# Sums of w_out split in other units of a Hymba block, with the first pair's gate products earlier on GpSimd

## The chip, the cores and the metric

The kernel runs on one core of a Trainium2 chip, alone. The metric is the time of one execution in device microseconds; three runs of the kernel before gave 958.17, 953.5 and 954.65 us, median 954.65. A profiled execution took 958.72 us, of which the profile's span is 956.9 us. Engines are named as in the profile: PE (TensorE matmul), PEld (its weight loads), DVE (VectorE), ACT (ScalarE), POOL (GpSimd), SP (the queue that issues the DMAs).

## The reference

One layer of a hybrid encoder. 16 meta tokens are prepended to a prompt of 256 tokens and to a sample of 2048; both go through the same layer in float32 (model width 1024).

```python
h = rmsnorm(z, norm_w)
proj = einsum('bld,de->ble', h, w_in)             # 1024 -> 2816
q, k, v, g_att, c_val, c_glu, g_conv = split(proj)
q = rmsnorm(q per head, q_norm_w); k = rmsnorm(k per head, k_norm_w)
att = windowed_gqa(q, k, v, sink) * silu(g_att)   # window 128, ALiBi, meta keys, sink
u = c_val * sigmoid(c_glu)
cnv = silu(layernorm(depthwise_conv31(u))) * silu(g_conv)
out = z + concat([att, cnv]) @ w_out              # 1024 -> 1024
```

## The kernel before

**Exact float32 by parts.** A float32 matrix product is made of three passes over parts of the operands: hi times hi, hi times lo and lo times hi. ACT casts the hi part and DVE subtracts it to get the lo part. Every weight and every activation that feeds PE goes through such a split.

**Stages.** The 2304 tokens and the 16 meta tokens are six groups of columns in two chunks of three groups. The input projection runs over eleven weight units of 256 columns, in the same order for each chunk: four conv units (U_C, value and gate), two units of the conv gate (U_GC), two of the attention gate (U_GA), one K/V unit (U_KV) and two Q units (U_Q). One unit and one group make PSUM tiles `pj`, each of 24 matmuls (L1020 for conv and gates, L1036 for K/V and Q). For K, GpSimd makes a reciprocal root (L179, L180), DVE multiplies it in (`kn`, L1194) and so frees the pj tile; PE transposes (`kt`). For Q, DVE makes `qs` (L1167) in the same way. SP loads the next activations `xt`, DVE scales them (L929), ACT and DVE or GpSimd split them into `xh` and `xl` (L948, L958).

**The depthwise convolution** is 31 taps for each conv unit and chunk, each one DVE instruction of 128x1167 (L1103). A planner meters them: `tick` gives PE time as credit, `owe` takes credit for other DVE work, and taps are issued from a queue while credit lasts. When all taps of a chunk are out, and LN_WAIT further steps of the planner's clock have gone by, its layer norms (`ln_block`) are issued.

**The output weights** w_out are needed as hi and lo rows and as sums and differences of rows (a product scheme that saves multiplications). `presplit_wo(e)` splits one row block and `presplit_sums(i)` makes one of two sets of seven operands: a cast on ACT (L394), a subtraction on DVE (L395), five more subtractions (L400) and seven stores of 512 KB to a DRAM buffer `wod`. The raw rows lie in four buffers of tag `xt`, which the activations use too, the operands in two of tag `xn`. `split_at` (L1347 to L1354) says beside which unit and group each of them is issued; `later(k)` puts a step k planner steps on.

**Attention and output.** The 18 blocks of 128 tokens are handled in steps of eight slots: scores S (L469), bias and maximum on DVE (L527), exponentials on ACT (L539), a normalisation on POOL (`pm` L556, `sb` L565), transposes of the probabilities on PE (`pT`, L585, L581), copies to `ptiles`, the product with V (`O`, L619). Blocks are paired for the output projection (`yb`, L725), whose operands are parts and sums of gated attention and gated convolution. `acts` (L758 to L781) lists for a pair p at which slot the gate tiles are loaded (`load_mix`: gc and cn, L446 and L448), when GpSimd multiplies them (`mix_conv`, L699), and when the parts are made (`two_parts`, L683 and L684). The first slots are spread through the last two Q units of chunk 1 (`spread`). `q_prep(a)` transposes the queries of block a (slot QSLOT = 6 of the step before).

**Order.** A scheduler orders each engine's queue, except those under a manual order: POOL from the opening of attention on (MAN1) and PE too in the rest (MAN2) keep the order in which the program is written. Each queue runs in its order; an instruction that waits holds all behind it. The pieces of w_out are loaded from `wod` (L438) into tiles that take over the buffers of xh and xl: wo0 and wo1 those of group 3, wo2 and wo3 those of group 4, which pj146 to pj148 read last.

Of the kernel before, what the change touches and what calls it, by code (L numbers as in the profile page):

```python
# [24 lines left out]
NB = NB_P + NB_S  # L25
# [20 lines left out]
CACHE = 2  # L46
WST = 9
W0 = 3
LN_WAIT = (9, 1)
LTAGS = "dbdbd" + "dcdcddddd"  # L50
LTAGS_N = len(LTAGS)
MAN1 = {mybir.EngineType.Pool}
# [1 line left out]
QSLOT = 6  # L54
# [27 lines left out]
NS = 2  # L82
# [34 lines left out]
CHUNKS = [[0, 1, 2], [3, 4, 5]]  # L117
U_C = [0, 1, 2, 3]
U_GC = [4, 5]
U_Q = [6, 7]  # L120
U_KV = 8
U_GA = [9, 10]
# [8 lines left out]
def hymba_kernel(  # L131
# [58 lines left out]
    def owe(ns):  # L190
        credit[0] -= ns

    def later(k, f):
        due.setdefault(clock[0] + k, []).append(f)
# [87 lines left out]
    vt, qt, q2t, sbt, pmt, gat, gct, cnt, att, opj = ({} for _ in range(10))  # L282
# [40 lines left out]
    vt, qt, q2t, sbt, pmt, gat, gct, cnt, att, opj = ({} for _ in range(10))  # L323
# [37 lines left out]
    def presplit_wo(e):  # L361

        raw = [sp.tile([P, 2, 400], F32, tag="xt", name=f"wor{e}_{nh}", bufs=XTB)[:, :, :UW] for nh in range(2)]
        for nh in range(2):
            src = w_out[e][:, 512 * nh : 512 * nh + 512].rearrange("p (a n) -> p a n", n=UW)
            nc.sync.dma_start(raw[nh], src)

        def split():
            hi = sp.tile([P, D], F32R, tag="xn", name=f"wohi{e}")
            if e < 4:  # L370
                owe(700)
            to = [wod[PIECES_W.index((e, hl))] for hl in range(2)]
            for nh in range(2):
                part = hi[:, 512 * nh : 512 * nh + 512].rearrange("p (a n) -> p a n", n=UW)
                nc.scalar.copy(part, raw[nh])
                nc.vector.tensor_tensor(raw[nh].bitcast(F32R), raw[nh], part, op=ALU.subtract)
                dst = to[1][:, 512 * nh : 512 * nh + 512].rearrange("p (a n) -> p a n", n=UW)
                later(1, lambda nh=nh, dst=dst: nc.sync.dma_start(dst, raw[nh]))
            later(1, lambda: nc.sync.dma_start(to[0], hi.bitcast(F32)))

        later(2, split)

    def presplit_sums(i):

        raw = {}
        for key, e, nh in ((11, 4 + i, 0), (21, i, 0), (12, 4 + i, 1), (22, i, 1)):
            raw[key] = sp.tile([P, 2, 400], F32, tag="xt", name=f"wor{key}_{i}", bufs=XTB)[:, :, :UW]
            src = w_out[e][:, 512 * nh : 512 * nh + 512].rearrange("p (a n) -> p a n", n=UW)
            nc.sync.dma_start(raw[key], src)

        def operand(name, key):
            both = sp.tile([P, D], F32R, tag="xn", name=f"wo{name}_{i}")
            hi, lo = (both[:, 512 * k : 512 * k + 512].rearrange("p (a n) -> p a n", n=UW) for k in range(2))
            nc.scalar.copy(hi, raw[key])  # L394
            nc.vector.tensor_tensor(lo, raw[key], hi, op=ALU.subtract)  # L395
            owe(700)
            later(1, lambda: nc.sync.dma_start(wod[PIECES_W.index((name, i))], both.bitcast(F32)))

        def minus(dst, x, y):
            nc.vector.tensor_tensor(raw[dst], raw[x], raw[y], op=ALU.subtract)  # L400
            owe(700)

        steps = (
            ("c1", 11, None),
            ("t1", 21, (11, 12, 11)),
            ("s4", 22, (12, 22, 12)),
            ("s1", 11, (22, 22, 11)),
            ("s3", 12, (21, 21, 22)),
            ("s2", 22, None),
            ("t0", 21, None),  # L410
        )

        def step(name, key, diff):
            operand(name, key)
            if diff:
                minus(*diff)

        for k, args in enumerate(steps):
            later(2 + k, lambda args=args: step(*args))
# [24 lines left out]
    def load_mix(b):  # L444
        gct[b] = pool["b"].tile([P, 4, P], F32, tag="gc", name=f"gc{b}", bufs=2)
        nc.sync.dma_start(gct[b], gd[4:8, :, P * b : P * b + P].rearrange("j p n -> p j n"))  # L446
        cnt[b] = pool["b"].tile([P, 4, P], F32, tag="cn", name=f"cn{b}", bufs=2)
        nc.sync.dma_start(cnt[b].rearrange("p j n -> p (j n)"), cd[b])  # L448

    def load_x(p, key):  # L450
        r, nh = key
        rows = NM + P * (2 * p + r)
        tc.keep_in_program_order(nc.sync.dma_start(yo(p, key), z[rows : rows + P, 512 * nh : 512 * nh + 512]))
# [222 lines left out]
    def parts(name):  # L676
        place, k = HOME[name]
        t = cst[place][:, k].rearrange("p (h e n) -> p h e n", h=2, n=P)
        return t[:, 0], t[:, 1]

    def two_parts(name, src):
        hi, lo = parts(name)
        nc.scalar.copy(hi, src)  # L683
        nc.vector.tensor_tensor(lo, src, hi, op=ALU.subtract)  # L684

    def with_rest(f):
        pending.append(f)
        while "rest" in cst and pending:
            pending.pop(0)()
# [8 lines left out]
    def mix_conv(b):  # L698
        nc.gpsimd.tensor_tensor(cnt[b], cnt[b], gct[b], op=ALU.mult)  # L699

    def mix_diff(p):
        nc.gpsimd.tensor_tensor(temp(0), cnt[2 * p + 1][:, 0:NS, :], cnt[2 * p][:, 0:NS, :], op=ALU.subtract)
        diff[p] = True
# [53 lines left out]
    for p in range(NB // 2):  # L757
        b0, b1 = 2 * p, 2 * p + 1  # L758
        for rel, f in (
            (5 - (p == 0), lambda b1=b1: load_mix(b1)),  # L760
            (6 - 2 * (p == 0), lambda b0=b0: load_mix(b0)),
            (9 + 3 * (p == 0), lambda p=p: load_x(p, (0, 1))),
            (11 - 2 * (p == 0), lambda b1=b1: mix_conv(b1)),
            (12 - 2 * (p == 0), lambda b0=b0: mix_conv(b0)),
            (13, lambda p=p: with_rest(lambda: mix_diff(p))),
            (12 + 2 * (p == 0), lambda p=p: load_x(p, (1, 1))),
            (13 - 2 * (p == 0), lambda b1=b1: two_parts("c1", cnt[b1][:, 0:NS, :])),
            (14, lambda: with_rest(lambda: two_parts("s3", temp(0)))),
            (17, lambda b0=b0: two_parts(("c", 0), cnt[b0][:, NS:4, :])),
            (17, lambda p=p: load_x(p, (0, 0))),  # L770
            (20, lambda b1=b1: two_parts(("c", 1), cnt[b1][:, NS:4, :])),
            (18, lambda p=p: load_x(p, (1, 0))),
            (18, lambda p=p: add_kept(p, (1, 1), 0)),
            (20, lambda p=p: add_kept(p, (0, 0), 1)),
            (21, lambda p=p: add_kept(p, (1, 0), 0)),
        ):
            acts.setdefault(16 * p + rel, []).append(f)
        for rel, name, es in JOBS:
            to = late_jobs if name == "s3" else jobs
            rel -= p == 0 and name == "c1"  # L780
            if p == LAST and name in ("t1", (1, 0)):  # L781
                for c0 in (0, 256):
                    to.setdefault(16 * p + rel, []).append((p, name, es, c0, 256))
            else:
                to.setdefault(16 * p + rel, []).append((p, name, es))

    def slot_step(s_, slot):
        a, bb = s_, s_ - 1
        has_a, has_b = a < NB, 0 <= bb < NB
        steps = PLAN if has_b else []  # L790
        if slot == 0:
            if a + 1 < NB:
                load_q(a + 1)
                load_k(a + 1)
        if slot == 1 and has_b and s_ > 1:
            load_ga(bb)
        if slot == VSLOT and 0 < a < NB:
            load_v(a)
        t = 8 * s_ + slot
        with_rest(lambda: None)  # L800
        for f in acts.get(t, ()):
            f()
        if slot < len(steps) and steps[slot]:
            bank(bb, *steps[slot])
        for job in jobs.get(t, ()):
            product(*job)
        if has_a:
            scores(a, slot // 4, slot % 4)
        if slot == QSLOT and a + 1 < NB:
            q_prep(a + 1)  # L810
        for job in late_jobs.get(t, ()):
            product(*job)
        tick(2400)
# [44 lines left out]
    if True:  # L858
# [483 lines left out]
        for n3 in range(3):  # L1342
# [4 lines left out]
        split_at = {  # L1347
            (0, U_C[0], CHUNKS[0][2]): lambda: presplit_wo(6),
            (0, U_C[1], CHUNKS[0][2]): lambda: presplit_wo(7),
            (1, U_C[0], CHUNKS[1][0]): lambda: presplit_wo(2),  # L1350
            (1, U_C[0], CHUNKS[1][2]): lambda: presplit_wo(3),
            (0, U_GA[0], CHUNKS[0][2]): lambda: presplit_sums(0),
            (0, U_KV, CHUNKS[0][0]): lambda: presplit_sums(1),
        }  # L1354

        for i, (c, u, g) in enumerate(items):
# [39 lines left out]
            if (c, u) == (0, ORDER[-1]):  # L1396
                p = preps[g + 3]
# [5 lines left out]
            if i == last_at[c, u] and u == U_GC[-1]:  # L1403
                def ready(c=c):
                    if left[c, 0]:
                        return False
                    seen.setdefault(c, clock[0])
                    return clock[0] >= seen[c] + LN_WAIT[c]

# [68 lines left out]
```

## Time and profile before

| | |
|---|---|
| Median of three runs | 954.65 us (953.5 to 958.17) |
| Profiled execution | 958.72 us |
| Its span | 956.9 us |
| Mean granted TensorE clock | 0.991 |
| DMA moved | 182.80 MB, mean 191 GB/s |

The page gives busy time for each engine and, in 40 slices of 23.9 us, how busy each was; a busy PE is an upper bound since its matmuls are pipelined. The view of waits names, for the waiting engine, the tile that waited and the instruction that released it: total us, times, longest. The windows give busy us and instruction counts of the engines in a stretch, then the granted clock as a share, the DMA share and GB/s. A timeline row has start, duration, engine, line, operation, tiles, shape and count, and in brackets the idle time before it and what ended it. Such rows follow in the prediction, beside the steps that use them.

### The profile page before, as it was taken

The numbers are of one execution on the slowest core, as the hardware profiler recorded it, in microseconds if no ns is written. First come the engines' busy times: TensorE is split into PE (matmuls) and PEld (weight loads), VectorE is DVE, ScalarE is ACT, GpSimd is POOL, SyncE is SP. The second block draws the span as 40 slices with busy tenths as digits, with TensorE's granted clock in tenths as the row PEclk, the third lists the DMA queues.
The fourth block names the chain that finished last, engine by engine and source line by source line (L and its number), as shares of the span: only waits on it lengthen the run. The fifth ranks groups of instructions, "written<-read, shape, count | busy, mean of one in ns | idle before, by whom it ended". The sixth has DMA issues, their size and how long they took to land.

```text
span 956.9 us, 16888 instructions
## 1 busy us (share of the span) xinstructions
PE 935.1 (98%) x5734; PEld 883.2 (92%) x5734; DVE 781.8 (82%) x1340; ACT 448.0 (47%) x1231; POOL 374.0 (39%) x553
## 2 busy tenths in 40 slices
PE   9999999999798999999999999999999999999998
PEld 8999999999698999999999999878888888888887
DVE  5579999988998859999997565668888887897884
ACT  7432112354446761011111346556676776776771
POOL 3320000165758620000000454658665455546554
PEclk9999999999999999999999999989999999999999
DMA  8574345779894642212333687996665665565431
GB/s 294 174 255 186 132 174 182 238 268 338 274 324 155 221 160 104 83 62 110 114 126 138 188 268 246 361 382 180 180 196 158 172 194 173 169 208 162 144 102 46
DMA packets 146342, 182.80 MB, mean 191 GB/s; under 512 B 40944, under 2 KB 106816, under 8 KB 146128
## 3 DMA queue, kind: packets, MB, share of 16 engines
q1 hardware_dynamic: 146256, 181.72, 58.1%
q8 instruction: 45, 0.74, 0.3%
q14 instruction: 41, 0.34, 0.1%
HBM read 115.83 MB, written 65.85 MB: 190 GB/s over the span
## 4 chain that ended last, share of the span: by engine, by line
PE 79%; DMA 7%; DVE 4%; POOL 4%; issue 3%; ACT 2%; SPq 0%; DVEq 0%; POOLq 0%; ACTq 0%
PE pj L1020 36%; PE yb L725 18%; PE pj L1036 8%; PE O L619 5%; PE S L469 4%; DMA xn<-in_z 2%; PE pT_m L585 2%; PE pT_c L585 1%; PE pT_x L585 1%; DMA wod<-wos 1%; DVE y L1103 1%; DVE xt L929 1%; DMA wraw<-in_w_in 1%; DMA xt<-in_zt 1%; PE warmup L1253 1%
## 5 line engine op out<-in xcount | busy, mean ns | idle before, releaser
L1020 PE MATMUL pj<-xh,ws 128*128 128x384 f32 (+1 forms) x1536 | 397.6, 339 | 0.3
L1103 DVE SCALAR_TENSOR_TENSOR y<-us,cw,y 128x1167 f32<-128x1167 f32 x240 | 329.6, 1432 | 0.3
L1020 PEld LDWEIGHTS pj<-xh,ws 128*128 128x128 f32 x1536 | 280.0, 188 | 0.8 <-DVE qs L1167 0.4
L1020 PE MATMUL pj<-xl,ws 128*128 128x384 f32 (+1 forms) x768 | 260.9, 340 | 0.1
L1036 PE MATMUL pj<-ws,xh 128*128 128x256 f32 (+1 forms) x880 | 168.2, 288 | 9.4 <-DVE kn L1194 5.7
L1036 PEld LDWEIGHTS pj<-ws,xh 128*128 128x128 f32 (+1 forms) x880 | 139.8, 191 | 10.7 <-issue 7.4
L1020 PEld LDWEIGHTS pj<-xl,ws 128*128 128x128 f32 x768 | 144.2, 188 | 0.5 <-DVE xl L958 0.4
L725 PE MATMUL yb<-wo,rest 128*128 128x512 f32 (+1 forms) x498 | 132.3, 399 | 0.0
L1036 PE MATMUL pj<-ws,xl 128*128 128x256 f32 (+1 forms) x440 | 126.4, 287 | 0.0
L725 PEld LDWEIGHTS yb<-wo,rest 128*128 128x128 f32 x498 | 87.1, 189 | 15.3
L1128 ACT ACTIVATE go<-pj 128x384 f32<-128x384 f32 x48 | 23.5, 490 | 147.9 <-PE pj L1020 139.5
L539 ACT ACTIVATE sb<-sb,nm 128x304 f32<-128x304 f32 (+5 forms) x144 | 77.8, 541 | 29.6 <-DVE nm L527 27.9
L565 POOL TENSOR_SCALAR sb<-sb,es 128x304 f32<-128x304 f32 (+5 forms) x144 | 73.1, 525 | 38.4 <-PE pT_x L585 18.8
L527 DVE CUSTOM_DVE_ANT_0 sb<-S,bias,vec 128x304 f32<-128x304 f32 (+5 forms) x144 | 74.3, 516 | 15.8 <-PE S L469 14.7
L179 POOL TENSOR_SCALAR ssk<-ssk 128x2 f32<-128x2 f32 x18 | 10.3, 571 | 191.5 <-ACT sqk L1142 191.0
L1036 PEld LDWEIGHTS pj<-ws,xl 128*128 128x128 f32 (+1 forms) x440 | 84.3, 192 | 0.4
L179 POOL TENSOR_SCALAR ssq<-ssq 128x4 f32<-128x4 f32 (+2 forms) x55 | 27.8, 506 | 115.7 <-ACT xn L883 89.5
L469 PE MATMUL S<-kw,q 128*128 128x304 f32 (+5 forms) x288 | 63.5, 302 | 2.8 <-ACT ptiles L601 2.2
L469 PEld LDWEIGHTS S<-kw,q 128*128 128x128 f32 x288 | 52.5, 188 | 13.6 <-ACT ptiles L601 2.4
L725 PE MATMUL yb<-wo,ptiles 128*128 128x512 f32 x216 | 60.8, 411 | 0.0
L647 POOL TENSOR_TENSOR at<-at,ga 128x256 f32<-128x256 f32 x36 | 26.6, 740 | 75.7 <-DVE at L641 75.7
L1063 ACT ACTIVATE sg<-pj 128x384 f32<-128x384 f32 (+1 forms) x24 | 11.8, 493 | 90.3 <-PE pj L1020 81.4
(162 smaller groups left out, 1489.5 us busy)
## 6 DMA issues: line engine op xcount, KB each, us to landing
wd<-ws SPq DMA_DIRECT2D x36, 512.0 KB, 5.8
ws<-wd SPq DMA_DIRECT2D x36, 512.0 KB, 5.7
wraw<-in_w_in SPq DMA_DIRECT2D x52, 256.0 KB, 6.3
xn<-in_z SPq DMA_DIRECT2D x18, 512.0 KB, 5.3
gd<-go SPq DMA_DIRECT2D x48, 192.0 KB, 2.3
wo<-wod SPq DMA_DIRECT2D x18, 512.0 KB, 6.8
yo<-in_z SPq DMA_DIRECT2D x36, 256.0 KB, 3.5
out_y<-yo SPq DMA_DIRECT2D x35, 256.0 KB, 2.5
```

The costliest lines, as they stand in the source:

```text
L179: nc.gpsimd.tensor_scalar(src, src, scale, eps, op0=ALU.mult, op1=ALU.add)
L469: r = f(*a, **k)
L527: nc.vector.tensor_tensor_reduce(out=sb[:, n, c0:c1], in0=ps[:, 0:w], in1=cst["bias"][:, kv, at + c0 : at + c1], scale=1.0, scalar=nsnk[:, ...
L539: nc.scalar.activation(sb[:, n, c0:c1], sb[:, n, c0:c1], AF.Exp, bias=nm[:, n : n + 1], scale=-1.0, accum_out=rs[:, n : n + 1],)
L565: nc.gpsimd.tensor_scalar(sb[:, k, a0:a1], sb[:, k, a0:a1], es[:, k : k + 1], 1.0, op0=ALU.mult, op1=ALU.mult)
L585: nc.tensor.transpose(pt[: c1 - c0, n, :], sbt[b, kv][:, n, c0:c1], ident)
L619: nc.tensor.matmul(opj[b, kv][:, n0:n1], t[:r, kv, :], p[:r, n0:n1], start=(k == "c" and i == 0), stop=(k == "x" and i == len(work) - 1),)
L647: nc.gpsimd.tensor_tensor(at[:, pr, :], at[:, pr, :], gat[b][:, pr, :], op=ALU.mult)
L725: nc.tensor.matmul(ps[:, :n], x[mi][:, i, :], w[wi], start=((name, e) in OPENS and k == 0), stop=(done and e == es[-1] and k == 2), skip_g ...
L1020: nc.tensor.matmul(ps[:, :n], ws[:, d, wi, P * half_i : P * half_i + P], x[xi][:, d, o : o + n], start=(k == 0), stop=(k == 3 * ND - 1),)
L1036: nc.tensor.matmul(ps[:rows, :UW], x[xi][:, d, o : o + rows], ws[:, d, wi, :], start=(k == 0), stop=(k == 3 * ND - 1),)
L1103: nc.vector.scalar_tensor_tensor(y[:, yo + o0 : yo + o1], u[:, o0 + k : o1 + k], cw[:, j, k : k + 1], y[:, yo + o0 : yo + o1], op0=ALU.mul ...
```

## The change

Four things. (1) The planner's wait before the layer norms is 7 instead of 9. (2) For the first pair alone (p == 0) both gate products are written in the same slot as the loads of their operands (slot 4, formerly 9 and 10), and the parts of `c1` two slots sooner. (3) The third q is transposed at slot 3 instead of 6. (4) The row splits 2 and 3 of w_out move from chunk 1's first conv unit to chunk 0's third; the sums' first set moves from chunk 0's first attention-gate unit to its fourth conv unit; the second set from chunk 0's K/V unit to chunk 1's second conv unit.

```diff
-LN_WAIT = (9, 1)
+LN_WAIT = (7, 1)
...
-            (11 - 2 * (p == 0), lambda b1=b1: mix_conv(b1)),
-            (12 - 2 * (p == 0), lambda b0=b0: mix_conv(b0)),
+            (11 - 7 * (p == 0), lambda b1=b1: mix_conv(b1)),
+            (12 - 8 * (p == 0), lambda b0=b0: mix_conv(b0)),
...
-            (13 - 2 * (p == 0), lambda b1=b1: two_parts("c1", cnt[b1][:, 0:NS, :])),
+            (13 - 4 * (p == 0), lambda b1=b1: two_parts("c1", cnt[b1][:, 0:NS, :])),
...
-        if slot == QSLOT and a + 1 < NB:
+        if slot == (3 if s_ == 1 else QSLOT) and a + 1 < NB:
             q_prep(a + 1)
...
-            (1, U_C[0], CHUNKS[1][0]): lambda: presplit_wo(2),
-            (1, U_C[0], CHUNKS[1][2]): lambda: presplit_wo(3),
-            (0, U_GA[0], CHUNKS[0][2]): lambda: presplit_sums(0),
-            (0, U_KV, CHUNKS[0][0]): lambda: presplit_sums(1),
+            (0, U_C[2], CHUNKS[0][0]): lambda: presplit_wo(2),
+            (0, U_C[2], CHUNKS[0][2]): lambda: presplit_wo(3),
+            (0, U_C[3], CHUNKS[0][1]): lambda: presplit_sums(0),
+            (1, U_C[1], CHUNKS[1][0]): lambda: presplit_sums(1),
```

No instruction is added or removed but four more table loads on ACT; the rest is a matter of order.

**ACT at the turn from K/V to Q in chunk 0, before** (wos: an operand of the sums, sqk and sqq: squares for the norms of K and Q, ks: a finished K):

```order
L394 CAST wos4_1_2449<-wor22_1_2259 128x512
L1185 CAST vs8_2548<-pj58_2516 128x2x64
L1142 ACTIVATE sqq0_0_2602,ssq0_0_2601<-pj59_2576 128x64 x2
L394 CAST wos1_1_2502<-wor11_1_2253 128x512
L1142 ACTIVATE sqq0_0_2602,ssq0_0_2601<-pj59_2576 128x64 x2
L1206 ACTIVATE ks5_2460<-kt5_2458,kscale_81 128x128
L1137 ACTIVATE sqq0_1_2651<-pj60_2625 128x256
L1206 ACTIVATE ks6_2512<-kt6_2510,kscale_81 128x128
L394 CAST wos3_1_2552<-wor12_1_2257 128x512
L1142 ACTIVATE sqq0_2_2692,ssq0_2_2691<-pj61_2666 128x64 x4
L394 CAST wos2_1_2611<-wor22_1_2259 128x512
```

The same place after the change:

```order
L1185 CAST vs8_2548<-pj58_2516 128x2x64
L995 CAST ws0_7_2563<-wraw10_3_2570 128x2x256
L1206 ACTIVATE ks5_2463<-kt5_2461,kscale_81 128x128
L1142 ACTIVATE sqq0_0_2598,ssq0_0_2597<-pj59_2572 128x64 x4
L1206 ACTIVATE ks6_2512<-kt6_2510,kscale_81 128x128
L1137 ACTIVATE sqq0_1_2645<-pj60_2619 128x256
L1142 ACTIVATE sqq0_2_2682,ssq0_2_2681<-pj61_2656 128x64 x4
```

The casts of the second set of sums are gone from between the norms of K and Q.

**SP and POOL where attention starts in chunk 1.** SP before: the loads of the gate tiles (gc, cn) of blocks 1 and 0, then the pieces of w_out (wa, wo):

```order
L446 DMA gc1_6235<-gd_64 128x4x128
L226 DMA qd_63<-qr0_17_6173 128x256
L448 DMA cn1_6237<-cd_70 128x512
L446 DMA gc0_6239<-gd_64 128x4x128
L448 DMA cn0_6241<-cd_70 128x512
L428 DMA wa0_6337<-wod_71 128x1024
L442 DMA ga0_6339<-gd_64 128x4x128
L438 DMA wo0_6360<-wod_71 128x1024 x2
```

SP after:

```order
L438 DMA wo0_6362<-wod_71 128x1024 x3
L438 DMA wo1_6409<-wod_71 128x1024
L277 DMA cd_70<-zn17_6135 128x512
L438 DMA wo1_6409<-wod_71 128x1024 x2
L438 DMA wo3_6630<-wod_71 128x1024
L438 DMA wo2_6573<-wod_71 128x1024 x3
L438 DMA wo3_6630<-wod_71 128x1024
L446 DMA gc1_6235<-gd_64 128x4x128
L448 DMA cn1_6237<-cd_70 128x512
L446 DMA gc0_6239<-gd_64 128x4x128
L448 DMA cn0_6241<-cd_70 128x512
```

The four gate loads went from ahead of all wo pieces to behind eleven of them, the last five of which go into the buffers of xh4 and xl4. POOL after the change, at the first normalisation of probabilities (pm, sb), which before had no L699 there (they stood behind the second sb):

```order
L526 MEMSET sb0_5804 128x32
L699 TENSOR_TENSOR cn1_6237<-cn1_6237,gc1_6235 128x512
L699 TENSOR_TENSOR cn0_6241<-cn0_6241,gc0_6239 128x512
L556 TENSOR_TENSOR pm0_0_6253<-sb0_5804,es0_0_6072 128x128
L565 TENSOR_SCALAR sb0_5804<-sb0_5804,es0_0_6072 128x176
L565 TENSOR_SCALAR sb0_5804<-sb0_5804,es0_0_6072 128x208
```

The two products now stand ahead of the first block's normalisation.

**PE at the first transposes of probabilities (pT0), before:**

```order
L1036 MATMUL pj148_6475<-ws1_7_5606,xl4_3258 128x256
L1036 MATMUL pj148_6475<-ws1_7_5606,xh4_3257 128x256 x2
L585 MATMUL pT0_c_0_6447<-ident_72,sb0_5876 128x128
L1036 MATMUL pj148_6475<-ws1_7_5606,xl4_3258 128x256
L1036 MATMUL pj148_6475<-ws1_7_5606,xh4_3257 128x256 x2
L585 MATMUL pT0_c_0_6447<-ident_72,sb0_5876 128x128
```

After:

```order
L1036 MATMUL pj150_6576<-ws1_7_5545,xh5_3500 128x256
L469 MATMUL S1_0_1_6520<-kw1_5796,q2_1_6351 128x240 x2
L469 MATMUL S1_0_2_6565<-kw1_5796,q2_1_6351 128x208 x2
L469 MATMUL S1_0_3_6613<-kw1_5796,q2_1_6351 128x176 x2
L469 MATMUL S1_1_0_6679<-kw1_5796,q2_1_6351 128x272 x2
L469 MATMUL S1_1_1_6698<-kw1_5796,q2_1_6351 128x240 x2
L585 MATMUL pT0_c_0_6449<-ident_72,sb0_5804 128x128
L585 MATMUL pT0_m_0_6515<-ident_72,sb0_5804 128x128
L585 MATMUL pT0_c_0_6449<-ident_72,sb0_5804 128x128
```

Before, the transposes were interleaved with the projection tiles pj148 to pj150; now they stand behind these and behind the second block's scores, and only pj151 is left for later.

## The prediction

> **What bounds the kernel now.** The page's busy line comes first, with the slices of DVE and ACT below it.
>
> ```profile
> PE 935.1 (98%) x5734; PEld 883.2 (92%) x5734; DVE 781.8 (82%) x1340; ACT 448.0 (47%) x1231; POOL 374.0 (39%) x553
> DVE  5579999988998859999997565668888887897884
> ACT  7432112354446761011111346556676776776771
> ```
>
> TensorE leaves some 20 us of the span idle, and no edit takes a matmul away. So the change can win only from those idle microseconds and from time at a reduced clock, and it can lose by making new waits. The view of waits, for PE alone, says who holds it up:
>
> ```profile
> PE pj L1036 <- DVE kn L1194: 5.7, 1, 5.7
> PE pj L1036 <- DVE qs L1167: 3.7, 3, 2.1
> PE S L469 <- ACT ptiles L601: 2.2, 1, 2.2
> PE O L619 <- DVE ptiles L602: 1.6, 1, 1.6
> PE kt L1204 <- DVE kn L1194: 1.4, 1, 1.4
> PE kt-1_2153 L1204 <- DVE kn-1_2102 L1194: 0.5, 1, 0.5
> ```
>
> The kn and qs rows are the K/V and Q units of chunk 0: 7.6 + 3.7 = 11.3 us. The S and O rows (3.8 us) are the first pair of attention blocks. The windows around these places (columns: us; busy and instruction count of PE, PEld, DVE, ACT, POOL; granted clock; DMA share; GB/s):
>
> ```profile
> 225.00:260.00 35.00, 30.73 (x257) 30.05 (x255) 33.30 (x54) 18.15 (x82) 27.01 (x24) 1.00 0.89 297
> 260.00:264.00 4.00, 0.66 (x3) 0.69 (x4) 3.76 (x9) 0.07 (x1) 3.69 (x3) 0.50 1.11 328
> 264.00:268.00 4.00, 4.00 (x26) 4.00 (x26) 4.00 (x6) 0.00 (x0) 2.29 (x2) 0.68 0.87 271
> 315.00:360.00 45.00, 44.85 (x285) 44.19 (x284) 31.09 (x53) 32.58 (x72) 18.22 (x33) 1.00 0.54 188
> 600.00:610.00 10.00, 10.00 (x88) 10.00 (x87) 6.33 (x23) 6.46 (x23) 6.35 (x15) 1.00 1.00 351
> 616.00:620.00 4.00, 2.60 (x20) 2.09 (x18) 3.22 (x10) 2.78 (x10) 4.00 (x5) 1.00 1.09 380
> 620.00:624.00 4.00, 3.42 (x15) 3.12 (x16) 3.12 (x8) 2.27 (x8) 2.99 (x10) 0.70 1.03 406
> ```
>
> In the K/V unit (225 to 260) DVE is busy 33.30 of 35 us; outside it TensorE has full cover. The transition to attention (600 to 632) is the other tight place: PE is full until 610, and DMA runs at its limit of about 390 GB/s.
>
> **The sum's basis.** The profiled execution took 958.72 us (span 956.9); the median of the three runs is 954.65, 0.4% below. I add up differences in the trace and apply them to the median.
>
> **1. The sums leave K/V of chunk 0 (L394, L395, L400 of presplit_sums(1), and sums(0) just before).** The longest wait ends when kn of block 7 is made. The timeline of DVE from kn 6 to kn 7, of ACT, and of POOL there:
>
> ```profile
> 253.56 0.28 DVE L1194 TENSOR_TENSOR kn<-pj,rqk 128x128 f32<-128x128 f32 x1
> ...
> 262.91 0.48 DVE L1194 TENSOR_TENSOR kn<-pj,rqk 128x128 f32<-128x128 f32 x2
> ```
> ```profile
> 259.70 0.37 ACT L1206 ACTIVATE ks<-kt,kscale 128x128 fp32r<-128x128 f32 x1
> 271.23 0.62 ACT L394 CAST wos<-wor 128x512 fp32r<-128x512 f32 x1 [11.16 <-DMA wod<-wos]
> ```
> ```profile
> 255.04 2.71 POOL L179 TENSOR_SCALAR ssk<-ssk 128x2 f32<-128x2 f32 x1 [2.79 <-ACT sqk L1142]
> 257.83 3.57 POOL L180 TENSOR_TENSOR rqk<-ssk,half 128x2 f32<-128x2 f32 x1
> ```
>
> The groups by line from 255 to 315 give the price of a tap and of an L996 (busy us, mean ns):
>
> ```profile
> L1103 DVE SCALAR_TENSOR_TENSOR y<-us,cw,y 128x1167 f32<-128x1167 f32 x14 | 20.0, 1428 | 0.0
> L996 DVE TENSOR_TENSOR ws<-wraw,ws 128x512 fp32r<-128x512 f32 x8 | 5.1, 688 | 0.0
> ```
>
> DVE spends 9.35 us from kn 6 to kn 7, on three taps, four L996, one L400 and two L395 among others. In the new order two taps, three L996 and one L1207 stand there: 2 x 1.43 + 3 x 0.69 + 0.3 = 5.2 us. The 5.7 us wait thus shrinks by 4.1. ACT's 11.16 us stop behind a store of the sums goes too; what is late next is the reciprocal root on POOL, above, which I don't let vanish. Of the other kn waits (1.9) I take away half, 1.0. The half clock from 260 to about 266.5 belongs to the long wait: granted 0.68 in 264:268 means 2.6 us at half speed with PE busy, a loss of 1.3, and 0.3 more before 264: 1.6 goes. Of the qs waits, DVE's loads of xt stood late because the sums held the same ring of four tiles:
>
> ```profile
> L929 DVE SCALAR_TENSOR_TENSOR xt<-xt,vec,bc 128x384 f32<-128x384 f32 x18 | 10.2, 607 | 2.0 <-DMA xt<-in_zt 2.0
> ```
>
> I take 1.3 of 3.7, since the xl work before the longer one stays. **Term: -8.0**, bounds -13 (all 11.3 and the clock) and 0 (the POOL chain alone decides).
>
> **2. Where the sums and presplit_wo(2), (3) go.** Units 2 and 3 of chunk 0 take sums(0) and both row splits, unit 1 of chunk 1 takes sums(1). One sum set is 12 DVE instructions of about 0.68 us, 8.2 us. In chunk 0 taps give way, and DVE's total before Q's end falls by sums(1). In 315:360 DVE has 14 us free, ACT 12. PE has no wait there now, and its pj ring is evacuated by ACT, which is under half busy in slices 4 to 12. **Term: 0**, bounds 0 and +3 (ACT's casts stop behind the stores, as at 271, in front of a sigmoid that frees pj).
>
> **3. The gate products go first on POOL (rel 9, 10 to 4, 4).** POOL follows the written order. Today it works like this:
>
> ```profile
> 603.49 1.74 POOL L565 TENSOR_SCALAR sb<-sb,es 128x176 f32<-128x176 f32 x4
> 605.32 0.19 POOL L179 TENSOR_SCALAR ssq<-ssq 128x4 f32<-128x4 f32 x1
> ...
> 610.40 1.02 POOL L180 TENSOR_TENSOR rqq<-ssq,half 128x4 f32<-128x4 f32 x1
> 613.17 0.40 POOL L556 TENSOR_TENSOR pm<-sb,es 128x128 f32<-128x128 f32 x1 [1.75 <-issue]
> ...
> 616.76 1.27 POOL L699 TENSOR_TENSOR cn<-cn,gc 128x512 f32<-128x512 f32 x1
> 617.97 0.12 POOL L526 MEMSET sb<- 128x32 f32 x1
> 618.06 1.39 POOL L699 TENSOR_TENSOR cn<-cn,gc 128x512 f32<-128x512 f32 x1
> ```
>
> Then the two L699 stand ahead of pm and of the first four L565. They need the loads of gc and cn. In the SP queue these loads stood ahead of all pieces of w_out, and now stand behind eleven of them, the last five of which (wo2, wo3) overwrite xh4 and xl4, so SP waits for pj148, their last reader. The PE rows:
>
> ```profile
> 608.72 0.28 PE L1036 MATMUL pj<-ws,xh 128*128 128x256 f32 x1
> 608.84 0.60 PE L585 MATMUL pT_m<-ident,sb 128*128 128x128 f32 x4
> 626.09 1.55 PE L725 MATMUL yb<-wa,ptiles 128*128 128x512 f32 x6
> 631.16 0.43 PE L469 MATMUL S<-kw,q 128*128 128x176 f32 x2 [2.24 <-ACT ptiles L601]
> ```
>
> I replay it in today's times, where pj148 ends at 609.0. Five pieces of 0.524 MB and four loads of 0.262 MB are 3.67 MB; at 390 GB/s that is 9.4 us, with some 2 us of start and older pieces the last one lands at about 620.6. Products to 622.0, pm and the first L565 to 622.9. PE in its new order has pj149, pj150 and six S pairs before the first pT transpose: 60 matmuls x 0.114 (10.00 us / 88) = 6.8, so it arrives at 615.9 and **waits 7.0 us**. The second sb follows on POOL: rest of the four L565 to 624.3, the four rqq (605.32 to 611.4 today, 6.1 us) to 630.4, pm and L565 to 631.3; PE is back for it at about 627.8 (transposes 1.7, copies of ptiles 1.3, O and qT 1.9) and waits 3.5 again. After that transposes, copy, O, pj151 (2.8) and O once more: yb starts near 638.5 against 626.09, +12.4. The third q, transposed three steps sooner (QSLOT 6 to 3), takes away the 2.24 us wait at 631.16 and its 0.4 us of transposes are done: -2.6. So +9.8, and +0.2 for the clock. **Term: +10**, bounds +3 (PE's wait on POOL is nearly covered, because the loads land as early as today) and +14 (two more stretches at half clock, 1.7 each, and the waits as above). DVE's L684 behind the product stands ahead of two L527 of S1_1, inside the same wait.
>
> By the Trainium skill, "TensorE: Matmul & The Clock Gate", section "What's actually happening", the clock halves after an idle window of about 3.4 us. By that rule the new 7 us wait starts a stretch at half clock that today's waits of 2.24 us at most would not have had, and the sum would, as an estimate, be 1.5 to 3 us higher. The row above says otherwise: 620:624 was granted 0.70 with no wait longer than 1.58 us, so a thin stretch of transposes suffices, the transition pays it already, and I add only 0.2.
>
> **4. LN_WAIT 9 to 7.** In the order the last layer norms stand later all the same, since sums(1) displaces taps in chunk 1, and four table loads more stand on ACT:
>
> ```profile
> L274 ACT ACT_TABLE_LOAD x4 | 5.1, 1283 | 1.1 <-issue 1.1
> ```
>
> 4 x 1.28 = 5.1 us of ACT, which was busy 6.46 of 10 us in 600:610 and holds nothing PE needs within 5 us. **Term: 0**, bounds 0 and +2.
>
> **Sum:** -8.0 + 0 + 10 + 0 = +2.0; 954.65 + 2.0 = 956.7 us.
>
> **Rivals.**
> *The transition has its cover.* If gc and cn land before 610 as today, POOL loses only its 2.7 us of products, and some of that is hidden: term 3 is +1, and 954.65 - 8.0 + 1 = 947.6. For it: the L699 rows of today have no idle time ahead of them. Against: SP's order is fixed and its head waits for pj148. Chance 0.25.
> *The gate products block POOL in full* (slower). The price is decided by the landing of cn: from 616 on each microsecond delays the first transposes by one. With +14, and only the 4.1 and 1.0 won in K/V, 954.65 - 5.1 + 14 = 963.6. For it: SP's head wait. Against: the waits overlap with work at half clock that is paid already. Chance 0.18.
> *The change doesn't do what it says in K/V.* In the order DVE has 27 taps in K/V and Q instead of 23, POOL's 3.57 us root stays beside them, and the wait turns from DVE's queue to POOL: term 1 is -2.5, giving 954.65 - 2.5 + 10 = 962.2. For it: L179 and L180 took 2.71 and 3.57 us there. Chance 0.14. The Trainium skill, "SBUF — State Buffer", section "SBUF: two separate sides", says that a DVE instruction with two SBUF inputs and a GpSimd one that reads SBUF exclude each other for their whole length; the 3.57 us row beside a chain of such DVE rows agrees.
>
> **How the numbers follow.** Forecast 0.43, rivals 0.25, 0.18, 0.14. The forecast's own range is 951 to 962; the first rival reaches down to 945 and the last two up to 965, so the range is 946 to 965. About 0.5% (4.8 us) is what a measurement of this kernel can tell from no change, since its runs differ by that much: faster means below 949.9, slower above 959.4. Faster: the first rival and a little, 0.26. Slower: the last two and a tenth of the whole from the forecast's upper part, less their lower ends, 0.34. Within: 0.40.
>
> **What would show it.** Term 1: no ACT row at L394 between 200 and 315, and the 5.7 us row of waits on kn under 2. Term 3: cn landing about 11 us after pj148's end; an L699 row on POOL with a long idle ahead of it, and on PE the first pT_c with a wait of 5 to 8 us; no 2.2 us wait of S on ptiles. It is wrong if the first pT_c doesn't wait, if the K/V wait stays on POOL's rows, or if new waits stand on pj between 100 and 225 or 330 and 380.

## The result

The changed kernel is **slower** by 1.2%: 967.54 us (966.32 to 969.29, four runs) against 955.78 us (953.5 to 958.17, four runs), a ratio of 1.0124 with a 95% interval of 1.009 to 1.0158. The profiled execution took 966.43 us (span 964.6), 7.7 us more than that of before. The forecast was 956.7 us, with 946 to 965 as its range.

The view of waits for PE after the change (waiting tile and line, what released it: total us, times, longest):

```profile
PE pT_c L585 <- POOL sb L565: 12.3, 3, 10.4
PE lnu L271 <- DVE zn L265: 3.0, 3, 2.1
PE pj L1036 <- DVE qs L1167: 0.7, 1, 0.7
PE pj L1036 <- DVE kn L1194: 0.2, 1, 0.2
```

The waits on kn and qs went from 11.3 us to 0.9, and waits of 12.3 us on the normalised probabilities (sb), one of them 10.4 us long, came in their place. The windows after the change (busy and count of PE, PEld, DVE, ACT, POOL; granted clock; DMA share; GB/s):

```profile
225.00:260.00 35.00, 33.41 (x277) 32.52 (x276) 34.51 (x58) 13.05 (x65) 20.95 (x22) 1.00 0.59 173
608.00:614.00 6.00, 0.44 (x2) 0.25 (x2) 0.34 (x2) 0.66 (x4) 0.00 (x0) 0.64 1.06 380
620.00:625.00 5.00, 3.71 (x11) 2.16 (x10) 3.45 (x11) 2.31 (x7) 4.45 (x11) 0.50 1.09 364
...
630.00:635.00 5.00, 5.00 (x27) 4.68 (x28) 2.55 (x5) 1.52 (x5) 1.95 (x5) 0.64 0.08 26
```

In the K/V unit PE is busy 33.41 of 35 us (30.73 before). From 608 to 614 hardly anything runs but DMA (380 GB/s), and the clock is at half from 609.7 to 633.6.

PE's first matmul of chunk 1, in the timeline of before and then of after:

```profile
317.50 0.45 PE L1020 MATMUL pj<-xh,ws 128*128 128x384 f32 x1
```
```profile
305.73 0.34 PE L1020 MATMUL pj<-xh,ws 128*128 128x384 f32 x1
```

The change is 11.8 us ahead here. It loses all of it, and more, around the start of attention. There SP holds the loads of the gate tiles (gc, cn) behind w_out:

```profile
597.34 6.08 SPq L438 DMA_DIRECT2D wo<-wod  x7
603.76 0.37 SPq L446 DMA_DIRECT2D gc<-gd  x1
605.55 0.33 SPq L448 DMA_DIRECT2D cn<-cd  x1
606.78 0.37 SPq L446 DMA_DIRECT2D gc<-gd  x1
608.05 2.00 SPq L448 DMA_DIRECT2D cn<-cd  x1
```

The last issue, from 608.05, lands at 616.31. The loads of cn of the first pair by source line, before and then after (duration in ns, first and last start; time from issue to landing):

```profile
L448 SPq DMA_DIRECT2D cn<-cd x2: 428/470/512, 597.1 to 598.1; - x2
DMA to landing us min/median/max: 2.8/4.1/5.5
```
```profile
L448 SPq DMA_DIRECT2D cn<-cd x2: 326/1166/2005, 605.6 to 608.0; - x2
DMA to landing us min/median/max: 8.3/8.7/9.2
```

POOL, in its fixed order, stands still meanwhile:

```profile
614.93 1.26 POOL L699 TENSOR_TENSOR cn<-cn,gc 128x512 f32<-128x512 f32 x1 [22.22 <-DMA cn<-cd]
616.45 1.26 POOL L699 TENSOR_TENSOR cn<-cn,gc 128x512 f32<-128x512 f32 x1 [0.26 <-DMA wa<-wod]
617.67 0.58 POOL L556 TENSOR_TENSOR pm<-sb,es 128x128 f32<-128x128 f32 x1
618.35 1.75 POOL L565 TENSOR_SCALAR sb<-sb,es 128x176 f32<-128x176 f32 x4
...
626.76 1.79 POOL L565 TENSOR_SCALAR sb<-sb,es 128x176 f32<-128x176 f32 x4
```

The 22.22 us of idle time are POOL's one long wait on the loads of a gate product. And PE:

```profile
606.99 1.45 PE L469 MATMUL S<-kw,q 128*128 128x176 f32 x6 [0.36 <-DVE nm L527]
618.82 0.47 PE L585 MATMUL pT_c<-ident,sb 128*128 128x128 f32 x1 [10.38 <-POOL sb L565]
...
627.28 1.81 PE L585 MATMUL pT_c<-ident,sb 128*128 128x128 f32 x4 [1.63 <-POOL sb L565]
...
635.65 1.63 PE L725 MATMUL yb<-wa,ptiles 128*128 128x512 f32 x6
```

yb starts at 635.65, against 626.09 before: a lead of 11.4 us at the K/V unit of chunk 1 (515.7 against 527.1) has become a lag of 9.6.

### The profile page after: what moved, and what is told of

It is laid out like the page before. It is cut to its first block, busy times and chain, and to the rows that moved or that the text cites. A ratio compares the mean times of both kernels' runs of the same rounds, so it can differ in the third digit from the quotient of the medians.

```text
span 964.6 us, 16883 instructions
## 1 busy us (share of the span) xinstructions
PE 937.1 (97%) x5734; PEld 880.8 (91%) x5734; DVE 784.1 (81%) x1340; ACT 453.9 (47%) x1235; POOL 371.9 (39%) x553
## 4 chain that ended last, share of the span: by engine, by line
PE 79%; DMA 7%; POOL 5%; DVE 4%; issue 2%; ACT 1%; SPq 1%; POOLq 0%; DVEq 0%; ACTq 0%
PE pj L1020 37%; PE yb L725 17%; PE pj L1036 9%; PE O L619 5%; PE S L469 3%; PE pT_m L585 2%; PE pT_c L585 2%; DMA kd<-ks 1%; PE pT_x L585 1%; DMA wo<-wod 1%; POOL sb L565 1%; DMA cd<-zn 1%; POOL rqq L180 1%; DVE xt L929 1%; DVE y L1103 1%
## 5 line engine op out<-in xcount | busy, mean ns | idle before, releaser
L1036 PE MATMUL pj<-ws,xh 128*128 128x256 f32 (+1 forms) x880 | 165.8, 287 | 1.1 <-DVE qs L1167 0.7
L725 PEld LDWEIGHTS yb<-wo,rest 128*128 128x128 f32 x498 | 86.9, 189 | 15.3
L179 POOL TENSOR_SCALAR ssk<-ssk 128x2 f32<-128x2 f32 x18 | 10.4, 577 | 207.7 <-ACT sqk L1142 207.6
L179 POOL TENSOR_SCALAR ssq<-ssq 128x4 f32<-128x4 f32 (+2 forms) x55 | 34.6, 629 | 91.7 <-ACT xn L883 70.0
L736 DVE TENSOR_TENSOR yo<-yb,yo 128x512 f32<-128x512 f32 (+1 forms) x55 | 37.1, 674 | 15.5 <-PE yb L725 15.3
```

What stands on the lines that cost most here:

```text
L179: nc.gpsimd.tensor_scalar(src, src, scale, eps, op0=ALU.mult, op1=ALU.add)
L725: nc.tensor.matmul(ps[:, :n], x[mi][:, i, :], w[wi], start=((name, e) in OPENS and k == 0), stop=(done and e == es[-1] and k == 2), skip_g ...
L736: nc.vector.tensor_tensor(y, ps[:, :n], y, op=ALU.add)
L1036: nc.tensor.matmul(ps[:rows, :UW], x[xi][:, d, o : o + rows], ws[:, d, wi, :], start=(k == 0), stop=(k == 3 * ND - 1),)
```

## The experiments

Twelve runs, one of them (e8) the kernel before for a second time. The table gives stretches of PE's timeline in us (from the first matmul of K/V in chunk 0 to the first of chunk 1; from the first of K/V in chunk 1 to the first yb; from there to the end), the start of chunk 1's first layer norm and the landing of the second cn, both counted from the start of K/V in chunk 1, then the median and the ratio, with its interval, to runs of before made beside it. Waits and time at half clock can fall on either side of the first yb: in e1 the clock is at half from 614.6 to 621.4, ahead of it, in e6 from 616.3 to 623.2, behind it. So the two stretches beside yb are read together.

| kernel | K/V 0 to chunk 1 | K/V 1 to yb | yb to end | layer norm at | cn landed at | median us | ratio |
|---|---|---|---|---|---|---|---|
| before | 98.0 | 99.0 | 330.8 | 20.4 | 76.4 | 955.78 | 1 |
| after | 86.9 | 120.0 | 329.0 | 29.2 | 100.6 | 967.54 | 1.0124 (1.009 to 1.0158) |
| e1 | 86.9 | 106.3 | 327.9 | 29.2 | 100.6 | 952.41 | 0.998 (0.9967 to 0.9993) |
| e2 | 97.2 | 100.9 | 330.7 | 20.4 | 76.5 | 957.45 | 1.0029 (1.0012 to 1.0046) |
| e3 | 95.0 | 96.6 | 333.6 | 17.5 | 72.1 | 956.33 | 1.0016 (0.9999 to 1.0033) |
| e4 | 87.4 | 107.7 | 328.5 | 29.3 | 103.5 | 952.58 | 0.9979 (0.9966 to 0.9992) |
| e5 | 87.6 | 105.0 | 331.1 | 29.2 | 86.8 | 955.28 | 1.0001 (0.9986 to 1.0016) |
| e6 | 86.9 | 95.7 | 333.3 | 17.4 | 71.3 | 948.33 | 0.9932 (0.9912 to 0.9952) |
| e7 | 87.5 | 97.7 | 333.5 | 17.5 | 73.2 | 947.45 | 0.992 (0.9903 to 0.9936) |
| e8 | 97.0 | 97.1 | 329.5 | 20.4 | 75.7 | 953.83 (one run) | |
| e9 | 87.6 | 96.3 | 334.4 | 17.5 | 72.5 | 948.28 | 0.9932 (0.9912 to 0.9952) |
| e10 | 89.5 | 97.1 | 330.8 | 20.4 | 75.4 | 950.44 | 0.9941 (0.9922 to 0.996) |
| e11 | 87.0 | 120.5 | 328.9 | 29.2 | 100.9 | 967.49 | 1.0145 (1.0114 to 1.0177) |
| e12 | 87.2 | 98.1 | 333.3 | 17.4 | 73.5 | 949.01 | 0.993 (0.9908 to 0.9952) |

### e1: after, with the products late again

```diff
-            (11 - 7 * (p == 0), lambda b1=b1: mix_conv(b1)),
-            (12 - 8 * (p == 0), lambda b0=b0: mix_conv(b0)),
+            (11 - 2 * (p == 0), lambda b1=b1: mix_conv(b1)),
+            (12 - 2 * (p == 0), lambda b0=b0: mix_conv(b0)),
...
-            (13 - 4 * (p == 0), lambda b1=b1: two_parts("c1", cnt[b1][:, 0:NS, :])),
+            (13 - 2 * (p == 0), lambda b1=b1: two_parts("c1", cnt[b1][:, 0:NS, :])),
```

> The kernel after, with the first pair's gate products back in their old slots (mix_conv at 9 and 10, c1 at 11). SP still loads gc and cn behind eleven pieces of w_out. Theory A (POOL is held by the products, which wait for late loads): the 10.4 us wait of pT on sb goes, the 11.4 us won before 520 stay, time 943 to 949. Rival B (the late loads and late layer norms cost by themselves): most of the loss stays, 960 or more. Rival C (products first on POOL cost wherever their loads stand): as A here.

952.41 us: 15 us less than after (14 by the ratios). POOL normalises at once and the products wait for cn alone, behind the second sb:

```profile
601.88 1.74 POOL L565 TENSOR_SCALAR sb<-sb,es 128x176 f32<-128x176 f32 x4
610.30 1.78 POOL L565 TENSOR_SCALAR sb<-sb,es 128x176 f32<-128x176 f32 x4
615.97 1.27 POOL L699 TENSOR_TENSOR cn<-cn,gc 128x512 f32<-128x512 f32 x1 [2.50 <-DMA cn<-cd]
```

The 10.4 us wait is gone, but the time isn't the 943 to 949 of theory A: K/V 1 to yb still takes 7 us more than in before (3 of them come back behind yb), with waits of lnu on zn of 3.4 us. Rival B holds for a part: late layer norms and late gate loads together cost something without the early products.

### e2: before, with only the products early

The lines of e1 the other way round, in the kernel before.

> The kernel before, with only the products moved first (mix_conv at 4 and 4, c1 at 9). SP here still loads gc and cn ahead of all pieces of w_out. Theory A: the loads land near 600 as before, POOL loses at most its 2.7 us of products, time within 3 us of 955.8. Rival C: POOL is held and the time is 965 or more. Rival B: 955.8.

957.45 us, 1.0029 of before: the products first on POOL cost some 3 us (1 to 4 by the interval) where their loads are early. POOL in e2:

```profile
599.11 1.29 POOL L699 TENSOR_TENSOR cn<-cn,gc 128x512 f32<-128x512 f32 x1 [3.82 <-DMA cn<-cd]
602.28 1.29 POOL L699 TENSOR_TENSOR cn<-cn,gc 128x512 f32<-128x512 f32 x1 [1.88 <-DMA cn<-cd]
603.52 0.41 POOL L556 TENSOR_TENSOR pm<-sb,es 128x128 f32<-128x128 f32 x1
604.03 1.74 POOL L565 TENSOR_SCALAR sb<-sb,es 128x176 f32<-128x176 f32 x4
```

sb is normalised from 604.03 here and from 603.49 in before. Rival C falls.

### e3: after, with the second set of sums back in K/V of chunk 0

```diff
-            (1, U_C[1], CHUNKS[1][0]): lambda: presplit_sums(1),
+            (0, U_KV, CHUNKS[0][0]): lambda: presplit_sums(1),
```

> The kernel after, with the second set of sums back beside K/V of chunk 0. In the queue order gc and cn then stand ahead of the w_out pieces again. Theory A: no long wait of pT on sb though the products stay first; part of the K/V wait comes back (3 to 8 us of the 11.4 won), 947 to 954. Rival C: the long wait stays, 968 or more. Rival B: as A.

956.33 us. The gate loads land early, no wait of pT on sb is left, and part of the K/V wait is back, in four smaller pieces instead of one:

```profile
PE pj L1036 <- DVE kn L1194: 5.7, 4, 1.8
```

It's 2 us over the upper end of what theory A expected: sums(1) alone is worth 8.1 of the 11.1 us won in K/V and Q (95.0 against 86.9), sums(0) and the row splits would be the rest. Against before, the profile wins 3.0 us in K/V and Q and 2.4 up to yb and gives 2.8 back behind yb.

### e4: before, with the four splits moved and the third q early

The edits of e1, without LN_WAIT (9 as in before).

> The kernel before, with only the four splits of w_out moved and the third q transposed at slot 3 (LN_WAIT 9, products late). Theory A: as e1, within 2 us of it, 943 to 949; LN_WAIT is worth under 1 us. Rival B: 960 or more. If LN_WAIT matters, it differs from e1 by over 3 us.

952.58 us, within 0.2 us of e1: LN_WAIT of 7 in chunk 0 is worth nothing that shows. Both miss the expected 943 to 949 alike.

### e5: after, with the gate loads pinned ahead of w_out

```diff
+        dma = nc.sync.dma_start(t.bitcast(F32), wod[i])
+        if idx in KEEP:
+            tc.keep_in_program_order(dma)
...
+        if b < 2:
+            tc.keep_in_program_order(dma)
```

The first is in load_wo (KEEP covers wo0 to wo3), the second in load_mix for gc and cn. The lines of e5 stand 7 below those of after.

> The kernel after, with the loads of gc and cn of the first pair and those of wo0 to wo3 pinned to the order in which they are written, so that SP issues gc and cn straight behind the last store of the layer norms and all wo pieces later. Products stay first on POOL, sums(1) stays in chunk 1. Theory A (the products wait for loads that stand behind w_out): the 10.4 us wait of pT on sb falls under 3, time 952 to 958. Rival D (the late layer norms keep the buffers of gc and cn occupied, so the loads are late whatever the queue): the wait stays over 6, 962 or more.

955.28 us, 12 us less than after, with the products still first on POOL:

```profile
601.67 1.29 POOL L706 TENSOR_TENSOR cn<-cn,gc 128x512 f32<-128x512 f32 x1 [7.38 <-DMA cn<-cd]
604.40 1.29 POOL L706 TENSOR_TENSOR cn<-cn,gc 128x512 f32<-128x512 f32 x1 [1.44 <-DMA cn<-cd]
605.65 0.40 POOL L563 TENSOR_TENSOR pm<-sb,es 128x128 f32<-128x128 f32 x1
606.16 1.75 POOL L572 TENSOR_SCALAR sb<-sb,es 128x176 f32<-128x176 f32 x4
```

PE no longer waits for the first sb. So it's the queue position of the loads that made the 10.4 us. The layer norms are as late here as in after; that they account for the 955 instead of e7's 947 isn't shown, since the pinned order puts the pieces of w_out later too.

### e6 and e7: the second set of sums written at K/V of chunk 1

```diff
-            (1, U_C[1], CHUNKS[1][0]): lambda: presplit_sums(1),
+            (1, U_KV, CHUNKS[1][0]): lambda: presplit_sums(1),
```

e6 has the products late (e1 with this line), e7 early (after with this line).

> As e1 (products late), but the second set of sums stands beside K/V of chunk 1, after the taps, instead of chunk 1's second conv unit. In the queue order the gate loads then stand ahead of w_out again. Theory A with the layer norms as the link: no wait of lnu or pT over 1 us between 560 and 620, K/V of chunk 0 stays free, 943 to 949. Rival E: the casts stop ACT among the norms of K in chunk 1 as they did in chunk 0, a wait on kn or qs of 3 us or more appears near 520 to 570, 953 or more.

> The kernel after, with only the second set of sums moved to K/V of chunk 1; products first on POOL. Theory A: loads are early, so the products cost what e2 showed, 2 to 3 us over e6: 945 to 952. Rival C (products first cost by themselves): 962 or more.

948.33 and 947.45 us: both beat before and after, and early or late products make no difference that can be told (the intervals overlap). SP in e6 issues the gate loads right behind the last store of the layer norms; the first two of the four:

```profile
579.64 0.40 SPq L277 DMA_DIRECT2D cd<-zn  x1
580.09 0.42 SPq L446 DMA_DIRECT2D gc<-gd  x1
580.56 0.65 SPq L448 DMA_DIRECT2D cn<-cd  x1
```

Rival E can't be judged as meant, since the sums do not run where they are written. One tile of the casts (L394) by duration, with first and last start, in after and then in e6:

```profile
L394 ACT CAST wot<-wor x4: 607/614/621, 90.5 to 335.4; 128x512 fp32r<-128x512 f32 x4
```
```profile
L394 ACT CAST wot<-wor x4: 608/615/622, 89.5 to 335.4; 128x512 fp32r<-128x512 f32 x4
```

In both the casts of the second set start from 321 to 335. In e6, where they are written beside K/V of chunk 1 (515.7), the scheduler pulls them forward by some 180 us, into a stretch where they cost PE little (chunk 1's start to its K/V takes 210.1 us, 209.6 before). The last tap ends at 525.3 in both, too. Yet the layer norms of chunk 1 begin 12 us apart; their first transposes, in after and in e6:

```profile
544.93 0.60 PE L252 MATMUL lnt<-ident,y 128*128 128x128 f32 x4
```
```profile
533.09 0.60 PE L252 MATMUL lnt<-ident,y 128*128 128x128 f32 x4
```

What differs is where the layer norms are written: behind the taps, whose issue the planner delays by the debt (`owe`) of the sums. e12 tries that alone.

### e8: before, once more

> The kernel before, unchanged, for a second profile. If the profile on which the prediction was made is typical, the waits on kn and qs sum to 10 to 12 us again and the span is 955 to 957; if they sum to under 9 us, part of the 11.4 us won by chunk 1's start was this one execution's.

The longest wait on kn is 5.7 us again and those on qs are 3.6 us, 9.5 us in all against 11.3, since the small waits on kn are nearly gone; K/V 0 to chunk 1 takes 97.0 us against 98.0. So most of what was won in K/V would be won on this profile too; about 1 us of it belongs to the first one. The second profile has a span of 952.0 against 956.9. The windows of the transition, first of the profile of before that the prediction used, then of e8:

```profile
620.00:640.00 20.00, 17.19 (x84) 14.87 (x85) 12.70 (x35) 11.63 (x34) 9.48 (x23) 0.83 1.06 391
```
```profile
620.00:640.00 20.00, 17.62 (x104) 15.13 (x103) 14.75 (x42) 13.37 (x38) 13.46 (x26) 1.00 1.06 391
```

With the same waits (2.2 and 1.6 us) the clock was granted in full here and to 0.83 there: K/V 1 to yb is 97.1 against 99.0 us.

### e9: e6, with the third q late again

```diff
-        if slot == (3 if s_ == 1 else QSLOT) and a + 1 < NB:
+        if slot == QSLOT and a + 1 < NB:
```

> As e6, with the third q transposed at slot 6 again. If that step was worth the wait of S on ptiles that the kernel before shows (2.2 us near 631), the wait is back and the time is 1 to 3 us over e6: 949 to 952. Rival: the wait belongs to the state of the transition, not to the slot, and the time equals e6 within 1 us: 947 to 949.

948.28 us, the same as e6. The wait of S on ptiles is back, and the one of yb on ptiles gets shorter (0.7 us instead of 2.5):

```profile
PE S L469 <- ACT ptiles L601: 2.1, 1, 2.1
```

The early third q moves a wait and saves nothing that shows in the time.

### e10: before, with the sums' second set written at K/V of chunk 1

One line of before changed: the key of presplit_sums(1) as in e6.

> The kernel before with one line changed: the second set of sums stands beside K/V of chunk 1 instead of chunk 0; sums(0), the row splits, LN_WAIT, products and q as before. By e3, where sums(1) alone was put back, that set costs about 8 us between the start of K/V and the start of chunk 1 (95.1 against 86.9 us there). Theory A: this one line wins most of it, 946 to 950, and chunk 1 starts 6 to 9 us earlier than in the kernel before. Rival F: sums(0), which ends just ahead of K/V, causes the wait with it, under 4 us are won, 951 to 955.

950.44 us: one line wins 0.6%, nearly as much as all the moves of e6 (0.7%), and K/V 0 to chunk 1 falls by 8.5 us (98.0 to 89.5; by 7.5 from e8's 97.0). Theory A holds for the stretch, and the time is just above its upper edge of 950. Rival F, under 4 us won, falls: 5.1 us are won in the median.

### e11: after, with PE kept busy in the wait

```diff
+        if (b, kv, n) == (1, 1, 1):
+            for _ in range(50):
+                nc.tensor.matmul(ps[:, 0:P], ident, ident, start=True, stop=True)
```

The result of these is overwritten by the scores.

> The kernel after, with 50 extra 128x128 matmuls of no use (their result is overwritten) ahead of the last scores before the first pT, so that PE works about 5.6 of the 10.4 us in which it waits for sb. POOL, SP and DVE keep their order, so sb is ready at the same time, some 618 to 619 us. Theory G (the long stretch at half clock after the wait, 23.9 us in the profile, is a second loss of about 6 us): the stretch gets shorter or goes and the time falls by 3 to 7 us, 960 to 964. Rival H (the clock costs little, the waits are all): the time stays within 1.5 us of 967.5 or grows.

967.49 us, no change. Each call became two instructions, so the 100 took 11.4 us and filled the wait. The windows of e11:

```profile
608.00:614.00 6.00, 6.00 (x56) 6.00 (x55) 0.00 (x0) 0.00 (x0) 0.00 (x0) 1.00 1.06 376
620.00:625.00 5.00, 2.37 (x9) 1.17 (x9) 3.29 (x10) 2.32 (x7) 4.53 (x10) 0.91 1.09 354
625.00:630.00 5.00, 3.89 (x13) 2.33 (x13) 2.71 (x5) 1.76 (x4) 4.58 (x10) 0.50 0.59 191
630.00:635.00 5.00, 5.00 (x25) 4.69 (x24) 2.81 (x5) 1.58 (x5) 2.23 (x6) 0.56 0.09 30
```

Half clock now starts at 624 instead of 610 and lasts 10.2 us instead of 23.9. The time doesn't follow: PE waits for POOL's second sb near 627 either way (1.63 us in after, 1.11 in e11). pj151, from 630 on, runs at half clock in both, so e11 doesn't show what that part costs. Theory G falls, rival H holds: the half clock up to 624 costs nothing that shows.

### e12: after, without the planner's debt for the second set

```diff
-            owe(700)
+            owe(700 * (i == 0))
```

Both calls in presplit_sums; nothing else differs from after.

> The kernel after with one thing changed: the planner books no debt (owe) for the second set of sums; its place in the program, the products and all else stay. In the profiles of after and e6 alike the casts of that set run from 320 to 335 and the last tap ends at 525.3, yet the first layer norm of chunk 1 starts at 544.9 in after and 533.1 in e6. Theory I (the late layer norms come from the planner's account, not from time on DVE): the layer norms start near 533 to 535, gc and cn are issued before 590, no wait of pT on sb over 2 us, time as e7, 946 to 950. Rival J (the work of the sums in chunk 1 itself delays them): the time stays over 960.

949.01 us, 0.993 of before, 18 us less than after by this edit alone. The first layer norm of chunk 1:

```profile
533.52 0.60 PE L252 MATMUL lnt<-ident,y 128*128 128x128 f32 x4
```

The casts run from 321 to 336 as in after. Theory I holds: it isn't the work of the sums that delays the layer norms but its entry in the planner's account.

## Why the prediction was wrong

**What bounds the kernel** was read rightly: the idle time in K/V and Q of chunk 0, and the transition.

**Term 1, -8.0.** The mechanism was right and the size too small: 98.0 to 86.9 us is -11.1, inside the bounds. The waits on kn were expected to keep 1.6 + 0.9 us and those on qs 2.4; they kept 0.2 and 0.7. By e8 about 1 us of the 11.1 was in the one profile used. The rival of the reciprocal root on POOL falls: in after the K/V wait is gone though a root of 2.97 us is still there and 31 taps, not 27, run between the starts of K/V and chunk 1.

**Term 2, 0.** Held: chunk 1's start to its K/V takes 210.0 us against 209.6.

**Term 3, +10, is the step that failed, by its size.** The queue order, POOL's stop, the wait of the first pT and the end of the wait at 631 came as worked out, and the second wait came with 1.6 us instead of 3.5. The mis-sized number is "with some 2 us of start and older pieces the last one lands at about 620.6", 11.6 us behind the end of pj148. The measured distance is 16.7 us (599.6 to 616.3). The six older pieces of w_out (wo0 and wo1) were issued only from 594.97 to 597.84 and landed from 598.6 to 606.8, with a store of the layer norms among them. So the queue came to the five that waited for pj148 some 7 us after its end, not two; these and the gate loads then took the 9.5 us that the sum gave them (9.4). The wait was 10.4 us instead of 7.0 (PE arrived 1.9 us later than assumed), and pj148 to yb took 36.1 us against 17.1 before, 19.0 instead of 12.4: 5.1 of the 6.6 us are the landing. The rest, 1.5, is about what pj151 lost at half clock (an estimate: 15 of its matmuls stand 0.21 us apart instead of 0.12). Behind yb 1.9 us came back (328.97 against 330.82 to the end), so the term is +17.1, beyond its bound of +14. Whether the third q did that, for which 2.6 us were taken off, isn't shown; in e9 its move saves nothing.

**The clock.** Of the Trainium skill's rule in "TensorE: Matmul & The Clock Gate", section "What's actually happening", that an idle window of about 3.4 us halves the clock, I set aside what it would add. After the change the trace has the clock at half from 609.7 for 23.9 us: it fell with the 10.4 us wait, but 1.3 us into it, before 3.4 us had been idle. e11 shows that the part up to 624 cost nothing; the part under pj151 is the 1.5 us above. So the 0.2 us in the sum was too little, and the 1.5 to 3 us set aside would have been nearer, at their lower end. e8 shows that before, which was said to pay for half clock in the transition already, doesn't always: its term isn't a property of the kernel.

**Term 4, 0.** It was +2.0: the layer norms, 9 us later after the start of K/V in chunk 1, hold PE at lnu, and the clock is at half for 3.4 us behind this wait (568.7 to 572.1):

```profile
567.87 0.66 PE L271 MATMUL lnu<-ident,zn 128*128 128x128 f32 x4 [2.12 <-DVE zn L265]
```

The reason given, that "sums(1) displaces taps in chunk 1", was wrong: the last tap ends at 525.3, earlier than before (540.5). The account displaced them in the program's text only (e12). The 2.0 is the difference from the start of K/V to the end of pj148 (83.9 us against 81.9), in which the wait is one item.

**The sum.** -11.1 + 0.4 + 17.1 + 2.0 = +8.4, against +7.7 between the two profiled executions (the other 0.7 us lie ahead of K/V in chunk 0). The medians differ by 11.8. The 4 us between are the basis: the profile of before, at 958.72, is 2.9 us above the median of its runs and that of after 1.1 below. Of the 4.9 us between the two profiles of before, 1.9 lie between K/V of chunk 1 and yb. A saving worked out on such a profile and applied to the median overstates. The miss would have been larger if term 1 had been right: it won 3.1 us more than forecast.

**The rivals.** What happened at the transition is the slower one, gate products that block POOL in full, at 967.5 instead of 963.6. Its price was made of two errors that partly cancel: 5.1 us won in K/V instead of 11.1, and +14, from the same mis-sized landing, instead of +17.1. "The transition has its cover" describes e12 and e7: 947.6 was its price, 947 to 949 their time. That is luck in part, since e7 wins 10.5 us in K/V and Q where the price has 8.0, and the basis was high.

That the loads' place in SP's queue makes the wait is shown by e5, that it takes the early products too by e1, that the debt puts the loads there by e12. That late layer norms and late loads together cost another 5 us or so without the wait is shown by e1 against e6; how that part divides between the two is left open. e6, e7, e9, e10 and e12 are faster than before by 0.6 to 0.8%, e1 and e4 by 0.2%; e7 has the lowest median.

## What to carry to other kernels

When work is moved in a kernel whose scheduler reorders queues, look at where the order puts it and not where the text does, and follow what the text's place does to the planner's own counts: here the moved work itself cost chunk 1 some 0.5 us, and its entry in the account delayed the layer norms by 12 us. Putting an instruction first on an in-order engine cost some 3 us (e2) or nothing that shows (e7) here where its operands were there, and 14 to 15 us where they weren't (after against e1): check its loads in the issuing queue, and count the pieces in flight ahead of them at the measured rate, all of them, from their own issue times. A gain that is worked out on a profile at the upper end of the runs should be held against a second profile first.

## What was not expected of the hardware

A float32 matmul of 128x128 by `ident` is two instructions of 0.114 us here (100 in 11.43 us), so filler cost twice what was planned. The clock fell to half in e11 at 624.1, after 13 us of nearly unbroken work and without a single wait over 1.3 us, in a stretch where PE was busy 2.37 of 5 us: a thinly filled stretch was enough here, without an idle one. And once at half it lasted until pj151 had run for some 3 us without a break (630.35 to 633.6 in after), though PE had been working again, with gaps, from 618.8.
